# Moving the first GLA head's turn, diagonal and later steps two positions later in a hybrid decoder block

## The chip, the cores and the metric

The kernel runs on one core of a Trainium2 chip. The core has five engines with a queue of instructions each: TensorE (PE in the profile, with its weight loads as PEld), VectorE (DVE), ScalarE (ACT), GpSimd (POOL) and SyncE (SP, which issues most transfers). An engine runs its queue in order; a tie between engines is a semaphore. The metric is the device time of one execution in microseconds; the median of three runs counts.

## The reference

One layer of a decoder: a mixer with two branches, and a gated feed-forward net with a causal convolution, in float32. 16 learned tokens stand ahead of the 1024 of the input, so T = 1040; the model is 1024 wide.

```python
proj = h @ w_in + b_in
# branch 1, GLA: 4 heads, keys and queries 128 wide, values 256 wide, per chunk:
bc = cumsum(log_a)
inter = (q * exp(bc)) @ S
scores[t, s] = sum_k q[t, k] * k[s, k] * exp(bc[t, k] - bc[s, k])      # s <= t
out = inter + scores @ v
S = exp(bc_last) * S + (k * exp(bc_last - bc)).T @ v
# branch 2, mLSTM: 4 heads, the same shape with scalar gates and a running maximum
y = sigmoid(gate_a) * (o_gla @ w_branch_gla) + sigmoid(gate_b) * (o_ml @ w_branch_ml)
h = h + y @ w_out, then the feed-forward net
```

## The kernel before

Products of the projections are split: weights and activations are each held as a high and a low part (wH, wL and xH, xL), and one product is three passes. Weight blocks are loaded into wr, rounded to wH on ACT and subtracted to wL on DVE (both L111 and L112, called a weight split here).

The first third of the kernel is the mixer. Its main stream is a row of projections: for every head the keys and queries (L195, three products of some 342 columns each, "thirds"), then the values (L238: pv_0 for the 16 learned tokens at L225, and pv_1 to pv_8 of 24 products, "blocks"). After head 7 come merge gates (gb). The stream runs through `main`. Beside it run the heads: `gla(s)` for heads 0 to 3 and `mlstm(s)` for heads 4 to 7, one after another in the list `side`, and `post(s)`, which flips a finished head, in the list `closing`. Each `yield` of the stream, one per block or third, adds 1.15 to a sum, and for every whole 1 in it `advance` lets each of the two lists run on to its own next `yield`. So the yields in `gla` say beside which block a piece of it is written; a yield more moves that piece and everything later on the side, the heads after it too. All of `gla` of head 0 but its first levels stands beside the values of head 0 and the keys and queries of head 1.

The written order is a wish: a planner puts the instructions of each engine in a row by their priorities and by when it takes their inputs to be ready. Evictions and weight splits have a higher priority (`hp`). `tc.issue_after(x)` ties instructions behind x, on the same engine's queue where both are there.

The steps of `gla` in order, with the names in the profile. `level(b)`: products of keys and queries with decays over spans of b (pk; exponential on ACT at L786), summed to sc_b on PE (L737, L708 for b = 1) and written to the score tile A by DVE (L754). `diagonal`: kq on DVE (L713), split on ACT (L701) and DVE (L702). `turn`: a product with the flip matrix turns half of A, sct (L727), and ACT copies it to An (L728). `scores_diagonal`: column sums of kq, sc_0 (L708), written by DVE (L721). `scores_large`: sc_32 and sc_64 (L737), written by ACT (L747). Then kh (L819 to L822: difference on DVE, exponential on ACT, product on DVE), qh (L834, L835), the transposes k0t and kt (L840 to L849), the next head's decay (`decay`: pre on PE at L668, la on ACT, bc with a scan on DVE at L681), u and up (L867, L860: state updates), omp, and four output products op (L898 with A or An, L899 with the state S), the states S_0 to S_6 made on DVE (L894).

PSUM, the memory that PE writes, has few buffers here: three named "s" shared by sc, sct, pre, k0t, kt, u, up and the flips ot and otm, three named "pj" shared by the projections, and two for op and omp. A product that takes a buffer waits until its last content has been read.

Of the kernel before, what the change touches and what calls it, by code (L numbers as in the profile page):

```python
# [17 lines left out]
P = 128  # L18
# [4 lines left out]
NK = D // P  # L23
# [4 lines left out]
DV = 256  # L28
# [17 lines left out]
def hybrid_kernel(ctx, tc, x, meta, norm_mix, w_in, b_in, gla_w_gate, gla_b_gate, gla_norm,  # L46
                  ml_conv_w, ml_conv_b, ml_norm, w_branch_gla, w_branch_ml, w_out, norm_ffn,
                  ffn_w_up, ffn_conv_w, ffn_conv_b, ffn_w_down, norm_final, out):
    nc = tc.nc
# [9 lines left out]
    def hp(n):  # L59

        return tc.high_priority(offset=max(1, min(n, tc.cur_priority - floor[0])))
# [140 lines left out]
    def together(*gens):  # L202
        gens = list(gens)
        while gens:
            for g in list(gens):
# [4 lines left out]
                    continue  # L210
                yield

    def proj_v(us, bB, vt):

        for u in us:
            U.get(u)
        for c in range(NC + 1):
            t0 = 0 if c == 0 else NM + P * (c - 1)
            n = NM if c == 0 else P
            pt = ps.tile([P, 512], F32, name=f"pv{us[0]}_{c}", tag="pj", bufs=3)  # L220
            i = 0
            if c == 0:
                for k in range(NK):
                    for b in U.got[us[k // 4]]:
                        nc.tensor.matmul(pt[:, :DV], xM[:, 48 * k:48 * k + P], b[:, k % 4, :],  # L225
                                         start=(i == 0), stop=(i == 2 * NK - 1))
                        i += 1
                with hp(PRI_E):
                    lo = hd.tile([NM, DV], F32, name=f"vlo{us[0]}", tag="junk", bufs=1)
                    nc.scalar.activation(lo, pt[32:48, :DV], AF.Copy)  # L230
                    nc.vector.tensor_tensor(lo, pt[:NM, :DV], lo, OP.add)
                    nc.vector.tensor_tensor(vt[:NM, 0, :DV], lo, bB[:NM, :], OP.add)
                yield
                continue
            for k in range(NK):
                wH, wL = U.got[us[k // 4]]
                for a, b in ((xH, wH), (xH, wL), (xL, wH)):
                    nc.tensor.matmul(pt[:, :DV], a[:, k, t0:t0 + P], b[:, k % 4, :],  # L238
                                     start=(i == 0), stop=(i == 3 * NK - 1))
                    i += 1  # L240
            with hp(PRI_E):
                nc.vector.tensor_tensor(vt[:n, c, :DV], pt[:n, :DV], bB[:n, :], OP.add)  # L242
            yield
# [212 lines left out]
    def key_query_proj(s):  # L456
        h = s % 4
        hh = heads.setdefault(s, {})
        if s < 4:
            pk = key_proj(s) if s != 1 else iter(())  # L460
            qT = hh["q"] = hd.tile([P, T + 3], F32, name=f"qT{s}", tag="q", bufs=2)
            pq = proj_cm(uq[s], TH_POST if s else SEG_POST, T0, lambda p, t0, n: nc.scalar.activation(
                qT[:, t0:t0 + n], p, AF.Identity, bias=cc(C_GQ + h), scale=QS))
            if s == 0:
                k1 = key_proj(1)
                yield from islice(together(pk, pq, k1), 6)
                yield from small_proj()
                token_sums(0, nc.sync)
                pkq = together(pk, pq)
                yield from islice(pkq, 1)  # L470
                decay(0)
                pack()
                yield from pkq
                side.append(gla(0))
                yield from k1
            else:
                yield from pk
                yield from pq
        else:
            kT = hd.tile([P, T + 3], F32, name=f"kT{s}", tag="k", bufs=2)  # L480
            qT = hd.tile([P, T + 3], F32, name=f"qT{s}", tag="q", bufs=2)
            hh["k"], hh["q"] = kT, qT
            for z, u, c in ((kT, uk[s], C_MK), (qT, uq[s], C_MQ)):
                nc.gpsimd.memset(z[:, 0:3], 0.0)
                yield from proj_cm(u, TH_ALL, 0, lambda p, t0, n, z=z, c=c: nc.scalar.activation(
                    z[:, 3 + t0:3 + t0 + n], p, AF.Identity, bias=cc(c + h)))

    def value_proj(s):
        bB = hd.tile([P, DV], F32, name=f"bB{s}", tag="bB", bufs=2)
        nc.sync.dma_start(bB, rowb(b_in, (O_GV if s < 4 else O_MV) + DV * (s % 4), DV))  # L490
        vt = hd.tile([P, NC + 1, DV + 1], F32, name=f"v{s}", tag="v", bufs=2)
        if s >= 4:
            nc.gpsimd.memset(vt[:, :, DV:DV + 1], 1.0)
        heads[s]["v"] = vt
        yield from proj_v(uv[s], bB, vt)
# [188 lines left out]
    def gla(s):  # L684
# [20 lines left out]
        def column_sums(pt, hl):  # L705

            for i, x in enumerate(hl):
                nc.tensor.matmul(pt.rearrange("p i n -> p (i n)"), ones, x, start=(i == 0), stop=(i == 1))  # L708

        def diagonal(g):  # L710

            k, q = (x.rearrange("p (i c t) -> p c i t", c=2, t=P)[:, g] for x in (kv, qv))
            nc.vector.tensor_tensor(raw.rearrange("p (i t) -> p i t", t=P), k, q, OP.mult)  # L713
            return split_raw(f"kq{s}_{g}")

        def scores_diagonal(kq):

            for g in range(2):
                pt = ps.tile([P, 4, P], F32, name=f"sc{s}_0_{g}", tag="s", bufs=3)
                column_sums(pt, kq[g])  # L720
                nc.vector.copy_predicated(An if g else A.rearrange("p (i c) t -> p i c t", c=2)[:, :, 0, :],  # L721
                                          lmask[0][:, None, :].to_broadcast([P, 4, P]), pt)

        def turn():

            pt = ps.tile([P, 4, P], F32, name=f"sct{s}", tag="s", bufs=3)
            nc.tensor.matmul(pt, flip, A.rearrange("p (i c) t -> p i c t", c=2)[:, :, 1, :], start=True, stop=True)  # L727
            nc.scalar.activation(An, pt, AF.Copy)  # L728
# [11 lines left out]
        def scores_large(pk, b):  # L740
            m = 64 // b
            pt = products(pk, b)
            for c in range(2):
                A2 = An if c else A.rearrange("p (i c) t -> p i c t", c=2)[:, :, 0, :]
                for n in range(m):
                    p0 = b * (m * c + n)
                    nc.scalar.activation(A2[2 * b * n:2 * b * n + b, :, 2 * b * n + b:2 * b * (n + 1)],  # L747
                                         pt[p0:p0 + b, :, p0:p0 + b], AF.Copy)
# [55 lines left out]
        with tc.issue_after(placed.ins) if placed else nullcontext():  # L804
            kq = [diagonal(0)]
        kq.append(diagonal(1))
        c, pk = made.pop(0)
        assert c == 32
        turn()
        yield  # L810
        scores_diagonal(kq)
        scores_large(pk, 32)
        (_, pk), = made
        yield
# [499 lines left out]
    def prod3(u, X, kouter, name, ahead=2, base=0):  # L1314
        wH, wL = U.get(u, ahead)
        pt = ps2.tile([P, 3, 512], F32, name=name, tag="big", bufs=2)
        XH, XL = X
        order = [(k, i) for k in range(NK) for i in range(3)] if kouter else [(k, i) for i in range(3) for k in range(NK)]
        for k, i in order:
            t0, n = TH_POST[i]  # L1320
            for a, b, j in ((wH, XH, 0), (wH, XL, 1), (wL, XH, 2)):
                nc.tensor.matmul(pt[:, i, :n], a[:, k, :], b[k][:, base + t0:base + t0 + n],  # L1322
                                 start=(k == 0 and j == 0), stop=(k == NK - 1 and j == 2))
        return pt[:, :, :342]
# [12 lines left out]
    for j in END:  # L1337
        pt = prod3(ugb[j], [[t[:, k] for k in range(NK)] for t in (xH, xL)], False, f"pe{j}", 0, T0)
# [12 lines left out]
    for j in range(NK):  # L1351
# [4 lines left out]
        pt = prod3(ubg[j], og, j < 2, f"bg{j}")  # L1356
# [17 lines left out]
    for j in range(NK):  # L1374
# [7 lines left out]
        pt = prod3(ubm[j], om_, j < 1, f"bm{j}")  # L1382
# [24 lines left out]
    for t in range(NC + 1):  # L1407
        a = r2.tile([P, T], F32, name=f"h{t}", tag=f"Y{t - 1}") if t else rb.tile([P, T], F32, name="h0", tag="T12")
# [222 lines left out]
    def po_bank(n, t, tag):  # L1631
        return psF.tile([P, 512], F32, name=f"po{n}_{t}", tag=tag)
# [5 lines left out]
    for i, tiles in enumerate(([1, 5, 2, 6, 0], [3, 7, 4, 8])):  # L1638
        for n in range(4):
# [13 lines left out]
            for it, t in enumerate(rest):  # L1653
                pt = po_bank(n, t, ("V1", "X1")[it % 2])
# [295 lines left out]
    i = FIRST  # L1950
    while i < len(seq):
        r, ph, m = seq[i]
        k = i % NP2
# [56 lines left out]
```

## Time and profile before

| | |
|---|---|
| median of 3 runs | 1873.1 us (1871.23 to 1874.72) |
| profiled execution | 1872.98 us, span 1871.3 us |
| mean granted clock of PE | 0.997 |
| PE busy | 99% of the span |
| DVE, ACT, POOL busy | 66%, 46%, 22% |
| DMA | 270 MB, 144 GB/s on average |

A row of the timeline gives the start in us, the length in us, the engine, the line and the operation with its tiles; the number behind x says how many instructions the row groups, and a bracket holds the idle time of the engine ahead of it and what ended that. The start of a PE row is where its first product began; products overlap, so the pitch from row to row is what counts, not the length. Head 0's turn is at 92 us, head 1's decay at 109 us, head 1's turn at 164 us, the last flips at 618 us.

### The profile page before, as it was taken

How to read it: one execution, taken by the hardware profiler on the slowest of the kernel's cores; microseconds unless marked ns; L12 is line 12 of the kernel's file. 1: busy time of each engine (PE TensorE's matmuls, PEld its weight loads, DVE VectorE, ACT ScalarE, POOL GpSimd, SP SyncE). 2: the span in 40 equal slices, each digit the busy share in tenths (PEclk: the TensorE clock that was granted, in tenths of full speed). 3: DMA queues.
4: the chain of work that ended last, by engine and by line, in shares of the span. 5: the costliest groups of instructions: out<-in, count | busy, mean ns of one | idle time of the engine just before them, and what ended most of it. 6: DMA issues, size and time to landing. Idle time of an engine off the chain costs nothing. (4 is left out here: it accounts for less than half of the span.)

```text
span 1871.3 us, 32608 instructions
## 1 busy us (share of the span) xinstructions
PE 1848.7 (99%) x13284; PEld 1771.3 (95%) x13284; DVE 1226.0 (66%) x1813; ACT 869.8 (46%) x1395; POOL 420.0 (22%) x476
## 2 busy tenths in 40 slices
PE   8999999999999999999999999999999999999998
PEld 7899999999999999999999999999999999987886
DVE  7766757554563466655532547698787788787876
ACT  6455555545454433432422335543443443465664
POOL 5201101205442000133281600012322222200100
PEclk9999999999999999999999999999999999999999
DMA  5111022143323855565973733334333334288894
GB/s 176 52 37 60 23 61 60 30 122 118 94 78 112 213 136 147 155 185 154 335 242 108 246 132 124 123 88 130 118 103 113 106 104 130 85 319 318 287 382 166
DMA packets 221600, 270.08 MB, mean 144 GB/s; under 512 B 13870, under 2 KB 176737, under 8 KB 221451
## 3 DMA queue, kind: packets, MB, share of 16 engines
q1 hardware_dynamic: 200603, 196.76, 34.0%
q0 software_dynamic: 18336, 62.56, 10.1%
q10 hardware_dynamic: 2512, 8.68, 1.2%
q8 instruction: 104, 1.70, 0.4%
q14 instruction: 45, 0.37, 0.1%
HBM read 198.36 MB, written 69.60 MB: 143 GB/s over the span
## 5 line engine op out<-in xcount | busy, mean ns | idle before, releaser
L546 POOL TENSOR_TENSOR ts<-ts 128x256 f32<-128x256 f32 x88 | 76.7, 877 | 45.2 <-DMA ts<-in_ffn_w_down_dram 43.3
L1529 POOL TENSOR_TENSOR SB<-SA,rg 128x512 f32<-128x512 f32 x20 | 32.7, 1635 | 240.0 <-issue 101.4
L238 PE MATMUL pv<-wH_mv,xH 128*128 128x256 f32 x256 | 74.8, 292 | 0.1
L238 PE MATMUL pv<-wH_gv,xH 128*128 128x256 f32 x256 | 74.6, 291 | 0.0
L788 POOL TENSOR_TENSOR pk<-pk,kT 128x256 f32<-128x256 f32 (+1 forms) x24 | 29.4, 1227 | 192.2 <-ACT pk L786 170.6
L1616 PE MATMUL po<-wH_wo,yH 128*128 128x256 f32 x256 | 72.5, 283 | 0.1
L238 PE MATMUL pv<-wH_gv,xL 128*128 128x256 f32 x256 | 72.1, 282 | 0.0
L238 PE MATMUL pv<-wL_gv,xH 128*128 128x256 f32 x256 | 72.1, 281 | 0.0
L1616 PE MATMUL po<-wL_wo,yH 128*128 128x256 f32 x256 | 71.7, 281 | 0.3 <-DVE wL_wo L112 0.3
L238 PE MATMUL pv<-wL_mv,xH 128*128 128x256 f32 x256 | 72.0, 281 | 0.0
L238 PE MATMUL pv<-wH_mv,xL 128*128 128x256 f32 x256 | 71.9, 281 | 0.0
L1616 PE MATMUL po<-wH_wo,yL 128*128 128x256 f32 x256 | 71.8, 281 | 0.0
L1564 DVE SCALAR_TENSOR_TENSOR cv<-u,fc,cv 128x1024 f32<-128x1024 f32 x44 | 65.1, 1482 | 0.4
L1511 POOL TENSOR_TENSOR A<-u2raw,A 128x512 fp32r<-128x512 f32 x20 | 42.5, 2124 | 86.2 <-ACT A L1510 86.2
L1322 PE MATMUL bg<-ogL,wH_bg 128*128 128x342 f32 x192 | 61.5, 320 | 0.0
L1322 PE MATMUL bg<-ogH,wH_bg 128*128 128x342 f32 x192 | 61.5, 320 | 0.0
L1322 PE MATMUL bm<-omH,wH_bm 128*128 128x342 f32 x192 | 61.4, 320 | 0.0
L1322 PE MATMUL bm<-omH,wL_bm 128*128 128x342 f32 x192 | 61.3, 319 | 0.0
L1322 PE MATMUL bg<-ogH,wL_bg 128*128 128x342 f32 x192 | 61.3, 319 | 0.0
L1322 PE MATMUL bm<-omL,wH_bm 128*128 128x342 f32 x192 | 61.2, 319 | 0.0
L242 DVE TENSOR_TENSOR v<-pv,bB 128x256 f32<-128x256 f32 x64 | 26.5, 418 | 39.2 <-PE pv L238 38.9
L1510 ACT ACTIVATE HA<-rg 128x1024 fp32r<-128x1024 f32 x16 | 17.0, 1060 | 73.0 <-PE Yu L1083 72.6
(787 smaller groups left out, 7523.0 us busy)
## 6 DMA issues: line engine op xcount, KB each, us to landing
gw<-in_w_in_dram SPq DMA_DIRECT2D x26, 512.0 KB
ts<-in_ffn_w_down_dram POOLq DMA_DIRECT2D x44, 256.0 KB, 3.9
tdn<-ts POOLq DMA_DIRECT2D x44, 256.0 KB, 3.1
rg<-in_ffn_w_up_dram SPq DMA_DIRECT2D x22, 512.0 KB
ru<-in_ffn_w_up_dram SPq DMA_DIRECT2D x22, 512.0 KB
adr<-s SPq DMA_DIRECT2D x40, 256.0 KB
rd<-in_ffn_w_down_dram SPq DMA_DIRECT2D x20, 512.0 KB
do<-tdn SPq DMA_DIRECT2D x18, 512.0 KB
```

Of the source, the lines that this page charges most:

```text
L238: nc.tensor.matmul(pt[:, :DV], a[:, k, t0:t0 + P], b[:, k % 4, :], start=(i == 0), stop=(i == 3 * NK - 1))
L242: nc.vector.tensor_tensor(vt[:n, c, :DV], pt[:n, :DV], bB[:n, :], OP.add)
L546: nc.gpsimd.tensor_tensor(t[:, o], t[:, a], t[:, b], OP.subtract)
L788: eng.tensor_tensor(e, e, k, OP.mult)
L1322: nc.tensor.matmul(pt[:, i, :n], a[:, k, :], b[k][:, base + t0:base + t0 + n], start=(k == 0 and j == 0), stop=(k == NK - 1 and j == 2))
L1510: nc.scalar.activation(h, src, AF.Copy)
L1511: eng.tensor_tensor(l, src, h.bitcast(F32), OP.subtract)
L1529: late.tensor_tensor(sb[:, 0:4], sa[:, 0:4], rg[:, 0:4], OP.subtract)
L1564: nc.vector.scalar_tensor_tensor(y, u[:, j:SEQ + j], fc[:, j, jj:jj + 1], y, OP.mult, OP.add)
L1616: nc.tensor.matmul(pt[:, :DV], a, b[:, k % 4, :], start=(k == 0 and i == 0), stop=(k == NK - 1 and i == len(terms) - 1))
```

## The change

`gla` of head 0 gets two yields ahead of the turn. `proj_v` keeps the last product it has written in `filled`, and for head 0 the turn and the diagonal's sums are tied behind the product that was last at that moment. For the heads after it nothing is changed in the code, but the two positions carry through the list to all of them. The instructions of every engine are the same set as before; lines behind the first edit have numbers higher by 2, behind the second by 7.

```diff
+    filled = []
     def proj_v(us, bB, vt):
...
-                    nc.tensor.matmul(pt[:, :DV], a[:, k, t0:t0 + P], b[:, k % 4, :],
-                                     start=(i == 0), stop=(i == 3 * NK - 1))
+                    filled[:] = [nc.tensor.matmul(pt[:, :DV], a[:, k, t0:t0 + P], b[:, k % 4, :],
+                                                  start=(i == 0), stop=(i == 3 * NK - 1)).ins]
...
         kq.append(diagonal(1))
         c, pk = made.pop(0)
         assert c == 32
-        turn()
-        yield
-        scores_diagonal(kq)
+        if s == 0:
+            yield
+            yield
+        with tc.issue_after(filled[0]) if s == 0 else nullcontext():
+            turn()
+        yield
+        with tc.issue_after(filled[0]) if s == 0 else nullcontext():
+            scores_diagonal(kq)
         scores_large(pk, 32)
```

First place, PE at head 0's turn. Before, from the last product of block 5:

```order
L238 MATMUL pv_5_1092<-wH_gv_1_608,xL 128x256
L727 MATMUL sct_1126<-A,flip 128x512
L708 MATMUL sc_0_0_1129<-kq_0_1119,ones 128x512 x2
L708 MATMUL sc_0_1_1133<-kq_1_1123,ones 128x512
L238 MATMUL pv_6_1146<-wH_gv_0_602,xH 128x256
L238 MATMUL pv_6_1146<-wL_gv_0_603,xH 128x256
L737 MATMUL sc_32_1137<-pk_32_1010 128x128 x4
L238 MATMUL pv_6_1146<-wH_gv_0_602,xL 128x256
L708 MATMUL sc_0_1_1133<-kq_1_1123,ones 128x512
```

After, from the last product of block 6, with block 7 cut out between its first and its last product:

```order
L240 MATMUL pv_6_1126<-wH_gv_1_608,xL 128x256
L729 MATMUL sct_1152<-A,flip 128x512
L240 MATMUL pv_7_1155<-wH_gv_0_602,xH 128x256
...
L240 MATMUL pv_7_1155<-wH_gv_1_608,xL 128x256
L710 MATMUL sc_0_0_1181<-kq_0_1119,ones 128x512 x2
L710 MATMUL sc_0_1_1185<-kq_1_1123,ones 128x512 x2
L739 MATMUL sc_32_1189<-pk_32_1010 128x128 x4
L240 MATMUL pv_8_1198<-wH_gv_0_602,xH 128x256
```

The turn has moved behind block 6, and the sums and sc_32 behind block 7, no longer among products of a block.

The same place on ACT. Before:

```order
L701 ACTIVATE kq_0_1119<-An_847 128x512
L701 ACTIVATE kq_1_1123<-An_847 128x512
L728 ACTIVATE An_847<-sct_1126 128x512
L834 ACTIVATE qh_1217<-bc_724 128x1024
L747 ACTIVATE A<-sc_32_1137 32x4x32 x2
L747 ACTIVATE An_847<-sc_32_1137 32x4x32 x2
L821 ACTIVATE kh_1172<-kh_1172 128x1040
```

After:

```order
L703 ACTIVATE kq_0_1119<-An_847 128x512
L703 ACTIVATE kq_1_1123<-An_847 128x512
L828 ACTIVATE kh_1224<-kh_1224 128x1040
L730 ACTIVATE An_847<-sct_1152 128x512
L841 ACTIVATE qh_1276<-bc_724 128x1024
L749 ACTIVATE A<-sc_32_1189 32x4x32 x2
L749 ACTIVATE An_847<-sc_32_1189 32x4x32 x2
```

The exponential of kh now stands ahead of the copy of the turn.

Second place, DVE at head 0's first state update (pre, la and bc are head 1's decay, wL_gk is the low part of a weight block, om belongs to the learned tokens' output). Before:

```order
L677 TENSOR_SCALAR bc_1274<-pre_694_1272 128x346
L680 TENSOR_TENSOR la_1267<-bc_1274,la_1267 128x1040
L894 SCALAR_TENSOR_TENSOR S_0_1365<-S_1320,dl_1182,up_0_1322 128x256
L681 SCALAR_TENSOR_TENSOR bc_1274<-rmask,la_1267 128x1040
L894 SCALAR_TENSOR_TENSOR S_1_1367<-S_0_1365,dl_1182,up_0_1322 128x256
```

After:

```order
L679 TENSOR_SCALAR bc_1333<-pre_694_1331 128x346
L682 TENSOR_TENSOR la_1326<-bc_1333,la_1326 128x1040
L683 SCALAR_TENSOR_TENSOR bc_1333<-rmask,la_1326 128x1040
L112 TENSOR_TENSOR wL_gk_1408<-wr_gk_1405,wH_gk_1407 128x1024
L885 COPY om_1377<-omp_1381 2x256
L901 SCALAR_TENSOR_TENSOR S_0_1391<-S_1372,dl_1234,up_0_1374 128x256
```

S_0 has moved behind the scan, a weight split and the copy of om. On PE, u, up_0, omp, up_1 and the first three products of op_0 stand one behind another there, after the last third of head 1's queries, where thirds stood between them before; pre stands between the second and the last third.

Third place, the end of the merge gates, ACT's queue (of are the flips' copies, gHA the first weight of the next stage, gb a merge gate). Before:

```order
L500 ACTIVATE gb_6182<-pj_342_6215 128x342
L639 ACTIVATE of_0_6241<-ot_0_0_6242,col 128x512
L639 ACTIVATE of_0_6241<-ot_0_1_6248,col 128x512
L1143 ACTIVATE gHA_0_6350<-gw_6346 128x1024
L500 ACTIVATE gb_6182<-pj_684_6258 128x342
L639 ACTIVATE of_1_6284<-ot_1_0_6285,col 128x512
```

After:

```order
L502 ACTIVATE gb_6173<-pj_342_6215 128x342
L1150 ACTIVATE gHA_0_6350<-gw_6346 128x1024
L502 ACTIVATE gb_6173<-pj_684_6241 128x342
L641 ACTIVATE of_0_6267<-ot_0_0_6268,col 128x512
L504 DMA gscb<-gb_6173 128x1026
L641 ACTIVATE of_0_6267<-ot_0_1_6275,col 128x512
L641 ACTIVATE of_1_6285<-ot_1_0_6286,col 128x512
```

The copies of the first half, ahead of the weight before, stand behind it and the last gate now; on PE all of the last head's flips stand behind the last third, where the first half stood ahead of that third.

## The prediction

> **What bounds the kernel now.** I read the engines' share first, then PE's waits, the timeline around the longest of them, and the granted clock there.
>
> ```profile
> PE 1848.7 (99%) x13284; PEld 1771.3 (95%) x13284; DVE 1226.0 (66%) x1813; ACT 869.8 (46%) x1395; POOL 420.0 (22%) x476
> ```
>
> PE is busy 99% of the span and the others far less. No work is added or removed, so the time can only move by what PE waits and by the clock it gets. PE's waits (us in total, times, longest):
>
> ```profile
> PE xtp L358 <- DVE xt L353: 3.5, 3, 2.9
> PE sct L727 <- DVE A L754: 2.7, 2, 2.3
> PE op L899 <- DVE S L894: 0.8, 1, 0.8
> PE sc L708 <- ACT kq L701: 0.7, 1, 0.7
> ```
>
> The first is the start-up, which is not touched. The second and fourth are head 0's turn and diagonal, the third is head 1's first output. The place of the second, PE alone (start, us, instruction, wait):
>
> ```profile
> 89.29 0.28 PE L238 MATMUL pv<-wH_gv,xL 128*128 128x256 f32 x1
> 91.90 1.78 PE L727 MATMUL sct<-A,flip 128*128 128x512 f32 x2 [2.33 <-DVE A L754]
> 95.55 0.80 PE L708 MATMUL sc<-kq,ones 128*128 128x512 f32 x1 [0.68 <-ACT kq L701]
> 99.11 0.28 PE L238 MATMUL pv<-wL_gv,xH 128*128 128x256 f32 x1
> ```
>
> Block 5 ends at 89.29 and the next steady product stands at 99.11. Between them lie the turn, four column sums, sc_32 and four products. The clock, in stretches of 3.41 us (PE busy is the second figure, PEclk the eighth column, after POOL):
>
> ```profile
> 88.83:92.24 3.41, 1.08 (x8) 0.83 (x7) 2.84 (x6) 1.06 (x1) 1.77 (x1) 1.00 0.00 0
> 92.24:95.65 3.41, 2.73 (x5) 0.67 (x3) 2.60 (x5) 1.38 (x3) 0.00 (x0) 0.50 0.00 0
> 95.65:99.06 3.41, 3.41 (x14) 3.22 (x15) 1.82 (x3) 1.94 (x4) 0.00 (x0) 0.50 0.00 0
> 191.23:194.64 3.41, 2.65 (x14) 2.06 (x13) 3.39 (x7) 1.15 (x5) 0.00 (x0) 1.00 0.00 0
> ```
>
> After a stretch with PE busy for 1.08 of 3.41 us (32%) the clock is 0.50 for two stretches; after one with 2.65 (78%) it stays 1.00. The Trainium skill, "TensorE: Matmul & The Clock Gate", section "HAM oscillation — how this bites in real kernels", asks only that no idle gap exceed some 3.4 us; this trace disagrees, for here a gap of 2.33 us is followed by half speed.
>
> **Part 1, the turn and the diagonal behind blocks 6 and 7: a gain.** What the same work takes at full speed shows in head 1:
>
> ```profile
> 163.75 1.02 PE L727 MATMUL sct<-A,flip 128*128 128x512 f32 x2
> 164.77 0.32 PE L195 MATMUL pj<-xL,wH_gk 128*128 128x348 f32 x1
> 168.44 1.10 PE L708 MATMUL sc<-kq,ones 128*128 128x512 f32 x4
> 169.37 1.05 PE L737 MATMUL sc<-pk 128*128 128x128 f32 x8
> 170.18 0.40 PE L195 MATMUL pj<-xH,wH_gk 128*128 128x346 f32 x1
> 102.28 0.36 PE L238 MATMUL pv<-wH_gv,xH 128*128 128x256 f32 x1
> 105.20 0.27 PE L840 MATMUL k0t<-ident,kh 128*16 128x128 f32 x1
> ```
>
> The turn is under 1.02 with one product in it, about 0.86; the sums 169.37 - 168.44 = 0.93; sc_32 170.18 - 169.37 = 0.81; a block of 24 products 105.20 - 102.28 = 2.92, so one is 0.12. Together 0.86 + 0.93 + 0.81 + 5 x 0.12 = 3.2, with a little at each switch 3.5. From 89.29 to 99.11 passed 9.82. The loss is 6.3: waits 2.33 + 0.68, and half of the 2.73 + 3.41 that PE was busy at 0.50, 3.1. Now block 6 stands behind block 5, so PE comes to the turn at 89.41 + 2.85 = 92.3, and A is there (next fence: 91.14 + 0.71 = 91.85). The wait goes with 0.4 to spare, and nothing is left to lower the clock at that place. Gain 6.3; bounds 5.9 (0.4 of wait stays) and 6.6.
>
> **Part 2, the copy of the turn behind the keys' exponential: a cost.** sc_32 takes the PSUM buffer that the turn filled, so it waits for ACT's An<-sct (L728). Before, ACT ran that ahead of qh and kh; now kh's exponential L821 stands ahead of it, and that needs L820, which DVE does behind L819 and the second kq.
>
> ```profile
> 91.14 0.71 DVE L754 COPY_PREDICATED A<-mu,sc 128x512 f32<-128x512 uint8 x1
> 95.01 1.22 DVE L819 TENSOR_TENSOR kh<-bc 128x1024 f32<-128x1024 f32 x1
> 96.14 0.69 DVE L702 TENSOR_TENSOR kq<-An,kq 128x512 fp32r<-128x512 f32 x1
> 99.87 0.15 DVE L820 TENSOR_TENSOR kh<-bc 128x16 f32<-128x16 f32 x1
> 95.53 0.60 ACT L728 ACTIVATE An<-sct 128x512 f32<-128x512 f32 x1
> 100.58 1.07 ACT L821 ACTIVATE kh<-kh 128x1040 f32<-128x1040 f32 x1
> 101.68 1.24 DVE L822 TENSOR_TENSOR kh<-kh,kT 128x1040 f32<-128x1040 f32 x1 [0.53 <-ACT kh L821]
> 96.74 0.73 DVE L721 COPY_PREDICATED A<-mu,sc 128x512 f32<-128x512 uint8 x1
> ```
>
> DVE's order up to the second kq is the old one, so that still ends at 96.83, L820 at 96.9, L821 at 98.0, the copy at 98.6. PE: turn until 93.15, block 7 until 96.05, the sums wait some 0.1 for the second kq and end at 97.1. sc_32 waits 98.6 - 97.1 = 1.5. Bounds: 0.7 if kh's chain runs one DVE instruction of 0.69 sooner, 2.2 if later by as much. I take 1.6 with the sums' 0.1. Until the copy, qh and the fills of sc_32 are late too; sc_64, a block later (98.6 + 0.8 + 2.9), finds its buffer read by then, since L822 and the two L721 behind the exponential take 1.24 + 2 x 0.73 from 98.0.
>
> **Part 3, head 0's first state update behind head 1's scan: a cost.** The decay products L668 move from ahead of all three query thirds to between the second and third. DVE then meets the scan L681 and the weight split wL_gk ahead of S_0, where S_0 stood ahead of the scan. Head 1 has this order already, but for the split:
>
> ```profile
> 183.85 0.64 PE L668 MATMUL pre<-raw_s,wgp 81*128 81x348 f32 x3
> 190.53 2.32 DVE L681 TENSOR_TENSOR_SCAN bc<-rmask,la 128x1040 f32<-128x1040 f32 x1
> 193.09 0.46 DVE L894 SCALAR_TENSOR_TENSOR S<-S,dl,up 128x256 f32<-128x256 f32 x1
> 193.60 0.70 PE L899 MATMUL op<-S,qh 128*128 128x256 f32 x2 [0.76 <-DVE S L894]
> 127.65 1.22 DVE L112 TENSOR_TENSOR wL_gk<-wr_gk,wH_gk 128x1024 fp32r<-128x1024 f32 x1
> 128.79 0.48 DVE L894 SCALAR_TENSOR_TENSOR S<-S,dl,up 128x256 f32<-128x256 f32 x1
> ```
>
> There PE was ready 193.60 - 0.76 - 183.85 = 9.0 after the decay products and S came at 9.75. The split adds 128.79 - 127.65 = 1.1: wait 0.76 + 1.1 = 1.9. Bounds 0.76 (the split costs nothing) and 2.3 (0.4 more for om, L878). On ACT the split's other half, wH_gk, waits for the last query product and is done before the scan is. Head 1 itself now has its 16 products of value block 0 (1.9 us) between, and a split of its own ahead of the scan: its 0.76 becomes some 0.4, bounds 0 and 0.8.
>
> **Part 4, the last head's flips: a cost.** Before, the first half stood ahead of the last merge-gate third and only the second half behind it. Now all stand behind it, and ot_1_0 needs the buffer of ot_0_0, which ACT reads behind a weight copy and a gate:
>
> ```profile
> 618.19 1.04 PE L637 MATMUL ot<-ident,or 128*128 128x128 f32 x8
> 619.30 0.42 PE L195 MATMUL pc<-xH,wH_gb 128*128 128x342 f32 x1
> 618.23 1.06 ACT L1143 ACTIVATE gHA<-gw 128x1024 fp32r<-128x1024 f32 x1 [3.16 <-PE pj L195]
> 619.20 0.44 ACT L500 ACTIVATE gb<-pj 128x342 f32<-128x342 f32 x1
> 619.53 0.68 ACT L639 ACTIVATE of<-ot,col 128x512 f32<-128x512 f32 x1
> ```
>
> PE has done three flips 619.30 - 618.19 = 1.1 after the third's end; ACT's read is done 619.53 + 0.68 - 618.19 = 2.0 after. Cost 0.9, bounds 0 (ACT takes the read first) and 1.3 (the next flip waits too).
>
> **The rest of the move.** Everything later on the side (levels of heads 1 to 3, all of heads 4 to 7, the flips) comes two positions later. Head 1 then stands about as head 2 stood, head 2 as head 3, where the waits list above has nothing but 0.4 at head 3's turn (2.7 - 2.3), so I put these at 0, bounds -0.4 and +1. On SP the stores of finished heads stand behind weight loads, and POOL's queue changes by three rows; no listed wait of PE names either, cost 0.
>
> **Sum.** -6.3 + 1.6 + 1.9 - 0.4 + 0.9 = -2.3, best -6.6 + 0.7 + 0.8 - 0.8 - 0.4 = -6.3, worst -5.9 + 2.2 + 2.3 + 1.3 + 1 = +0.9. The profiled execution took 1872.98 (span 1871.3 and 1.7 around it), 0.1 below the median 1873.1. So 1870.7, between 1866.7 and 1873.9 with the clock full.
>
> **Rivals.**
> *The new waits halve the clock.* Part 2 leaves PE busy 1 - 1.6/3.41 = 53% of a stretch, part 3 leaves 44%. The trace has 32% halved and 78% kept, so the limit may lie on either side; and a wait may be cut in two by a stretch's border. One halving costs about the 3.1 of part 1: 1873.8. Both: 1876.9, slower than before; it decides once the limit lies above 53% and each wait falls within one stretch. By the skill's rule of 3.4 us neither wait would halve the clock, and the time would stay 1870.7.
> *The new waits are smaller.* If ACT and DVE get the copy and S_0 done in time, parts 2 and 3 go to their lower bounds and the time is 1867 to 1869. Against it: both waits follow from an order of instructions on one engine, which cannot be overtaken.
> *The change does not do what it says.* The turn still waits for A, if A's chain is later than 92.3: at most the margin's loss, some 1 us, 1871.7. The rows of DVE up to A are in the old order, so I think it unlikely.
> *A level of head 1 or 2 comes late.* With two more weight splits (1.22 each) ahead of the last level in head 1, its turn could wait 2 us and halve the clock: 1870.7 + 2 + 3.1 = 1875.8. A of head 1 in the kernel before:
>
> ```profile
> 159.59 0.72 DVE L754 COPY_PREDICATED A<-mu,sc 128x512 f32<-128x512 uint8 x1
> ```
>
> It was done at 160.3 and the turn came at 163.75, so there is room of 3.4 us for two splits.
>
> **How the numbers follow.** As worked, clock full: 0.42. New waits smaller: 0.19. The turn still waits: 0.03. One halving: 0.14. Both: 0.12; a late level with its halving: 0.10. About 0.2% (3.7 us) is what a measurement of this kernel can tell from no change: faster means under 1869.4, slower over 1876.8. The first case lies mostly inside (0.06 of it below), the second below, the third and fourth inside; the last two lie about the upper border, 0.2 of their 0.22 above once something else goes wrong with them. Faster 0.25, same 0.55, slower 0.20. Leaving out one in ten at each end gives 1867.3 to 1877.5.
>
> **What would show it.** Right: no wait at the turn, PEclk 1.00 from 88 to 100; sc_32 waiting 1.5 for ACT's An; op's second S product waiting 1.9 at head 0; ot_1_0 waiting 0.9. Wrong: PEclk 0.50 behind either wait, or a wait in heads 1 to 3 that this list lacks.

## The result, and the profile after

The changed kernel takes 1882.3 us (median of five runs, 1882.1 to 1884.1) against 1873.1 (1871.2 to 1874.7): ratio 1.0052, 95% interval 1.0041 to 1.0063. The forecast was 1870.7 within 1867.3 to 1877.5, so it is outside, on the slow side. The profiled execution, with a span of 1882.4 us against 1871.3, is the slowest of the five; the medians lie 9.2 us apart, the two traces 11.1.

PE's waits after (us in total, times, longest):

```profile
PE u L997 <- ACT of L641: 7.6, 1, 7.6
PE xtp L360 <- DVE xt L355: 3.4, 3, 2.8
PE sc L739 <- ACT An L730: 2.2, 2, 1.5
...
PE op L906 <- DVE S L901: 1.7, 1, 1.7
PE sc L739 <- ACT of L641: 1.2, 1, 1.2
...
PE ot L639 <- ACT of L641: 0.9, 1, 0.9
...
PE pj L195 <- DVE v L244: 0.7, 1, 0.7
```

The wait at head 0's turn is gone, the expected new waits (sc at An, op at S, ot at of) are there, and the list is headed by one that the forecast did not have: u, the first state product of head 7, waits 7.6 us for a copy of head 6's flips. At that place (POOL, ACT and PE of the timeline, in order of time):

```profile
569.15 0.40 PE L195 MATMUL pj<-xH,wH_gb 128*128 128x342 f32 x1
569.39 1.51 POOL L542 DMA_DIRECT2D ts<-in_ffn_w_down_dram  x2
573.44 0.60 PE L639 MATMUL ot<-ident,or 128*128 128x128 f32 x4
575.64 0.72 POOL L548 TENSOR_TENSOR ts<-ts 128x256 f32<-128x256 f32 x1 [4.74 <-DMA ts<-in_ffn_w_down_dram]
579.76 0.69 POOL L550 DMA_DIRECT2D tdn<-ts  x1 [0.30 <-POOL ts L548]
582.60 0.46 ACT L502 ACTIVATE gb<-pj 128x342 f32<-128x342 f32 x1 [12.79 <-DMA tdn<-ts]
582.95 0.68 ACT L641 ACTIVATE of<-ot,col 128x512 f32<-128x512 f32 x1
583.78 1.19 PE L997 MATMUL u<-v,K 16*128 16x257 f32 x2 [7.60 <-ACT of L641]
```

ts is a background tile: beside the last heads POOL loads a part of the next stage's down weights into it, makes sums and stores them as tdn. It has the name "gst" and a single buffer, and the first merge gate gb takes the same buffer. So ACT's first copy of gb cannot start before the store of ts has landed, 582.6; ACT had been idle for 12.79 us. Behind it on ACT stands the copy of the flip (ot of 573.44), and u needs the PSUM buffer that this copy frees. The same places before:

```profile
563.82 1.45 POOL L540 DMA_DIRECT2D ts<-in_ffn_w_down_dram  x2
571.50 0.69 POOL L548 DMA_DIRECT2D tdn<-ts  x1 [0.30 <-POOL ts L546]
571.59 0.70 PE L990 MATMUL u<-v,K 16*128 16x257 f32 x2
572.57 0.51 PE L195 MATMUL pj<-xH,wH_gb 128*128 128x342 f32 x1
576.77 0.46 ACT L500 ACTIVATE gb<-pj 128x342 f32<-128x342 f32 x1 [3.75 <-PE pj L195]
```

There ACT waited for the projection and not for ts, and the flips' copies and u stood ahead of gb. The load has moved from 563.82 to 569.39, while the merge gate's first third, which belongs to the main stream, has not moved with it: it starts 3.4 us sooner, at 569.15 instead of 572.57, as less of the heads' work stands ahead of it. What starts the load is the end of head 6:

```profile
546.52 1.86 POOL L95 TENSOR_TENSOR rs6r<-rs6v,mhalf 128x9 f32<-128x9 f32 x1 [24.64 <-DVE rs6v L93]
```

is the row before, and the row after is:

```profile
553.10 1.83 POOL L95 TENSOR_TENSOR rs6r<-rs6v,mhalf 128x9 f32<-128x9 f32 x1 [28.20 <-DVE rs6v L93]
```

From there POOL runs sums of the tokens, their stores, and then the load, in both kernels. The load also took longer: POOL waited 4.74 us for it where it had waited 2.17 (the first of the tile's four sums began at 567.44 before and at 575.64 after).

The granted clock after, in stretches of 3.41 us (PE busy is the second figure, the clock stands after POOL):

```profile
96.54:99.95 3.41, 1.79 (x11) 1.08 (x10) 2.53 (x7) 2.58 (x3) 0.00 (x0) 0.99 0.00 0
99.95:103.36 3.41, 3.41 (x19) 3.41 (x18) 2.42 (x4) 1.30 (x6) 0.00 (x0) 0.51 0.00 0
123.84:127.25 3.41, 2.06 (x15) 2.01 (x16) 2.85 (x8) 1.89 (x7) 0.00 (x0) 1.00 0.44 125
577.77:581.18 3.41, 0.00 (x0) 0.00 (x0) 0.00 (x0) 0.00 (x0) 2.39 (x4) 1.00 0.28 97
581.18:584.60 3.42, 0.82 (x2) 0.50 (x2) 0.00 (x0) 1.03 (x2) 0.00 (x0) 0.50 0.21 74
584.60:588.01 3.41, 3.41 (x11) 2.93 (x11) 0.48 (x1) 0.39 (x1) 0.00 (x0) 0.50 0.34 138
```

The clock is halved behind sc_32's wait for one stretch (3.41 of busy PE, 1.7 lost) and behind u's for two (4.2 busy, 2.1 lost). All of the difference lies ahead of the next stage, whose first product pc stood at 619.30:

```profile
630.58 0.42 PE L195 MATMUL pc<-xH,wH_gb 128*128 128x342 f32 x1
```

630.58 - 619.30 = 11.3 us, where the spans differ by 11.1. Some 0.3 of it lies ahead of the change already, for the start-ups of two executions are not alike. Where traces are compared closely below, pc is therefore counted from the last level's sum ahead of head 0's turn, which all kernels share. Before and after:

```profile
85.68 1.05 PE L737 MATMUL sc<-pk 128*128 128x128 f32 x8
85.94 1.05 PE L739 MATMUL sc<-pk 128*128 128x128 f32 x8
```

From there to pc it is 533.6 us before and 544.6 after, 11.0 more.

### The profile page after: what moved, and what is told of

Same layout as the page of the kernel before. It is cut to its first block, busy times and chain, and to the rows that moved or that the text cites. A ratio compares the mean times of both kernels' runs of the same rounds, so it can differ in the third digit from the quotient of the medians.

```text
span 1882.4 us, 32597 instructions
## 1 busy us (share of the span) xinstructions
PE 1849.5 (98%) x13284; PEld 1772.8 (94%) x13284; DVE 1222.6 (65%) x1813; ACT 869.3 (46%) x1395; POOL 423.8 (23%) x476
## 4 chain that ended last, share of the span: by engine, by line
PE 81%; DVE 6%; DMA 4%; issue 4%; POOL 2%; ACT 2%; SPq 0%; POOLq 0%; ACTq 0%; DVEq 0%
PE pj L195 8%; PE Yu L1090 6%; PE Xu L1090 6%; PE Zu L1090 6%; PE pv L240 6%; PE bg L1329 5%; PE bm L1329 5%; PE Zg L1090 4%; PE Yg L1090 4%; PE Xg L1090 4%; PE po L1623 4%; PE Vu L1090 3%; PE pdX L1780 2%; PE pdZ L1780 2%; PE pdY L1780 2%
```

## The experiments

Times are medians beside runs of the kernel before on the same chip (1872.4 for e1 to e4, 1872.7 for e5 to e8); ratios are against those.

**e1, the background tile in another buffer.** "bc" is a single buffer too; it held the decays of heads 0 and 2, and after them the convolved queries qc of heads 4 to 7 lie in it.

```diff
-                                t = half_load(wp, "gst")
+                                t = half_load(hd, "bc") if s == 6 else half_load(wp, "gst")
```

> The changed kernel, with one thing other: head 6's background tile (ts of the down weights' sums, filled and emptied by POOL and its DMAs) lies in a buffer of its own kind that the GLA heads have left, and no longer in the single buffer that the merge gate's gb takes. The order of every engine is that of the changed kernel. Theory (the merge gate's first copy waits for that buffer, and u behind it for ACT): u's wait of 7.6 us and the half clock behind it (4.2 us of busy PE at 0.50, 2.1) go, 1882.3 - 9.7 = 1872.6. Rival (u waits because the heads' flips come too late for PSUM, whatever the buffer of gb): u still waits over 5 us, 1880 to 1882. Rival (the loss is at head 0, by its new waits and the clock): 1881 to 1882.

Measured 1873.6, ratio 1.0005 (0.9996 to 1.0015). u does not wait any more:

```profile
PE xtp L360 <- DVE xt L355: 3.5, 3, 2.9
PE sc L739 <- ACT An L730: 1.9, 2, 1.2
...
PE op L906 <- DVE S L901: 1.7, 1, 1.7
PE sc L739 <- ACT of L641: 1.2, 1, 1.2
```

The buffer is not one of the tile's own, as was expected: the load waits on POOL for 7.35 us, until head 7's products with qc (msc) have read it (the last ends at 573.50), and starts at 574.09. So the tile's last store is issued even later than in the changed kernel (579.76), and u runs at 573.43 without waiting for it:

```profile
573.43 0.70 PE L997 MATMUL u<-v,K 16*128 16x257 f32 x2
581.40 0.70 POOL L550 DMA_DIRECT2D tdn<-ts  x1 [0.30 <-POOL ts L548]
```

No engine's order was changed and no instruction left out, so gb's sharing of the buffer is the cause of u's wait, and with the clock behind it of about 9 us of the median. Both rivals fall: the flips stand where they stood in the changed kernel, and the new waits at head 0 are still there. One thing more differs in this trace, which the buffer does not explain: sc_32 waits 1.2, not 1.5, and the clock behind it stays full (1.7). From the last level's sum (84.94) to pc (618.27) it is 533.3 us, 0.3 less than before.

**e2, heads 4 to 7 put back.** The small rows' step between heads 3 and 4 has six empty yields; four are left.

```diff
-        for _ in range(6):
+        for _ in range(4):
             yield
         for g in range(3):
```

> The changed kernel, with two of six empty yields taken out of the small rows' step that stands between head 3 and head 4, so that heads 4 to 7 and their flips stand where they stood before the change, while heads 0 to 3 stay two positions later. Theory: everything of the loss that lies in heads 4 to 7 goes (7.6 + 2.1 at u, 0.9 at the last flips, 0.7 at head 4's keys), 1882.3 - 11.3 = 1871.0. Rival (the loss is at head 0 and in heads 1 to 3): 1880 to 1882.

Measured 1880.4, ratio 1.0038 (1.0023 to 1.0053): a miss. u's wait is gone as the theory has it, but two new ones have come, with two stretches of half clock beside them (385.04 to 391.87):

```profile
PE rtp L611 <- DVE of L653: 4.3, 1, 4.3
...
PE rtp L611 <- ACT of L641: 1.7, 1, 1.7
```

rtp are the small rows' transposes, which now meet a GLA head's late flips; the row of DVE ahead of that copy says what held it:

```profile
387.15 0.17 DVE L957 COPY gp<-WB 128x8 f32<-128x8 f32 x1 [7.16 <-DMA WB<-rsc]
388.66 0.21 DVE L653 TENSOR_SCALAR of<-otm,col 128x2 f32<-128x2 f32 x1
388.93 1.12 PE L611 MATMUL rtp<-ident,srst 128*128 128x128 f32 x4 [4.29 <-DVE of L653]
```

DVE stood 7.16 us at a load of head 4 (WB) with the flip's copy behind it. In the changed kernel DVE stands at the same load, for 7.72 us, but there the transposes come at 393.7, when the copy is done. The six yields stand ahead of the transposes, and with four of them the transposes come too soon. As a test of where the loss lies the run says only that u's wait goes with the late heads' place.

**e3, only heads 4 to 7 later.** The kernel before with eight yields in that step; head 0 is as it was.

> The kernel before, with two more empty yields in the small rows' step, so that only heads 4 to 7 stand two positions later, and head 0's turn is where it was. Theory: the whole loss without the gain, 1873.1 + 7.6 + 2.1 + 0.9 = 1883.7. Rival (the loss is at head 0 and in heads 1 to 3): 1873 to 1874.

Measured 1886.5, ratio 1.0067 (1.0052 to 1.0082), 2.8 more than the 1883.7 of the theory; in the trace u waits 1.3 longer than in the changed kernel, and the half clock behind it lasts three stretches instead of two, 0.8 more. The waits:

```profile
PE u L990 <- ACT of L639: 8.9, 1, 8.9
...
PE sct L727 <- DVE A L754: 2.2, 2, 1.8
...
PE ot L637 <- ACT of L639: 0.9, 1, 0.9
```

Head 0's old wait and its half clock stay, and the late heads alone bring u's, here 8.9. So the loss needs nothing of what was done at head 0's turn: the two positions, handed down the list to head 6, are enough.

**e4, head 0's copy of the turn first on ACT.**

```diff
+            copied[:] = [nc.scalar.activation(An, pt, AF.Copy).ins]
...
+        with tc.issue_after(copied[0]) if s == 0 else nullcontext():
             nc.scalar.activation(kh, kh, AF.Exp, scale=1.0 / 16)
```

> The changed kernel, with head 0's exponential of kh tied behind the copy of the turn on ACT, as those two stood before the change. If sc_32's wait of 1.5 us and the stretch of half clock behind it (3.4 us of busy PE at 0.50, 1.7) both come from that order: 1882.3 - 3.2 = 1879.1, and the clock is 1.00 from 95 to 106 us. If the half clock comes from something else: 1880.8.

Measured 1882.9, ratio 1.0052 (1.0037 to 1.0067): no gain over the changed kernel. Yet at head 0 it did what was expected, sc_32 waits no more and the clock is full there. Head 7's transposes, ahead of u, show it: in the changed kernel and in e4

```profile
568.41 0.27 PE L964 MATMUL k0t<-ident,kc 128*16 128x128 f32 x1
```

```profile
565.35 0.27 PE L966 MATMUL k0t<-ident,kc 128*16 128x128 f32 x1
581.37 1.19 PE L999 MATMUL u<-v,K 16*128 16x257 f32 x2 [8.26 <-ACT of L641]
```

3.06 us earlier, of 3.2 expected. At u 0.7 of it is given back, as its wait is now 8.26, and about 0.7 more, as the half clock behind it lasts three stretches (576.73 to 586.97, 5.6 us of busy PE) instead of two. So pc stands 1.8 earlier than in the changed kernel (628.79); the span is 0.7 shorter. Where the rest went behind pc is not settled: from pc to the end it is 1251.8 us in the changed kernel, 1252.9 in e4 and 1254.0 in e1, with no change there. The median shows no gain at all.

**e5, the buffer, the copies first in heads 0 to 2, and S_0 first.** e1 and e4's tie (for s < 3), and a priority for head 0's first state:

```diff
+                    with hp(3000) if s == 0 and c == 0 else nullcontext():
                         nc.vector.scalar_tensor_tensor(Sn[:, :DV], S[:, :DV], dl[:, c:c + 1], up[:, i, :], OP.mult, OP.add)
```

> The kernel with the background tile in a buffer of its own (e1), and two of the new waits taken away by order: in heads 0 to 2 the exponential of kh stands behind the copy of the turn on ACT, and head 0's S_0 is given a higher priority, which puts it ahead of the scan and of the weight split on DVE. Theory (with the buffer out of the way, what is left of the loss are the small new waits): sc_32's 1.2 and 0.7 (heads 0 and 2) and S_0's 1.7 go, e1's 1873.6 - 3.6 = 1870.0. Rival (such waits are only handed on): 1873 to 1874, as e1.

Measured 1870.1, ratio 0.9989 (0.9980 to 0.9998), faster than the changed kernel and, by 0.1%, than the kernel before. sc's wait for An is gone and S's is down to 0.4:

```profile
PE sc L739 <- ACT of L641: 1.2, 1, 1.2
...
PE op L909 <- DVE S L904: 0.4, 1, 0.4
```

From the last level's sum (85.35) to pc (615.49) it is 530.1 us, 3.2 less than in e1, and the waits are shorter by 1.2 + 0.7 + 1.7 - 0.4 = 3.2: with the buffer out of the way the small waits are worth their length, and are not handed on.

**e6, e5 and the next stage's weight copy behind the last flips.**

```diff
+            with tc.issue_after(flipped[7]) if 7 in flipped else nullcontext():
+                nc.scalar.activation(h, src, AF.Copy)
+            flipped.pop(7, None)
```

> e5, and ACT's first weight copy of the next stage, gHA, behind the copies of the last flips. If the last flips' 0.9 is worth its length: 1870.0 - 0.9 = 1869.1, with pc's first product 0.9 earlier than in e5. If gHA's products wait for it instead: 1870 to 1871.

Measured 1869.8, ratio 0.9986 (0.9977 to 0.9995), against e5 within the noise. ot's wait is down from 0.9 to 0.3, but pc stands at 615.69, not earlier than in e5: a wait of pj for kT has grown by as much (1.0 against 0.4), and from the last level's sum (84.94) pc comes 0.6 later, which is not explained. A product of the next stage (Xg) waits 1.4 us anew. So this small wait was not worth its length.

**e7, only head 6's flips later.** The kernel before, with five yields in place of three ahead of head 6's flips.

```diff
-        for _ in range(3 if s != 3 else 6):
+        for _ in range(5 if s == 6 else 3 if s != 3 else 6):
```

> The kernel before, with only head 6's flips two positions later. On POOL nothing changes its place: token sums, load, sums and stores of the background tile stand as before. Theory (the late thing is the background tile, whose chain hangs on head 6's end): u does not wait, 1872 to 1873. Rival (the flips are what comes too late for u's PSUM buffer): u waits 5 us or more, 1880.

Measured 1873.4, ratio 1.0006 (0.9997 to 1.0015), and u does not wait. Late flips of head 6 alone do not bring the wait. The run does not repeat the changed kernel's order, though: u stays at 571.48, ahead of gb (576.67) and of the last flip. That the late background tile is the cause is what e1 shows; in the changed kernel the flip's copy stands behind gb and gb needs the buffer.

**e8, one position instead of two.**

```diff
         if s == 0:
             yield
-            yield
```

> The changed kernel with one empty yield in place of two. Head 0's turn then still stands behind block 5, so its wait of 2.3 us stays, while everything later stands one position later. Theory: before, the buffer was free at 574.3 and wanted at 576.8, 2.5 us to spare; after, two positions, it was late by 7.6 (10.1 in all). One position takes about half of that: u waits some 2.5 us, 1872.4 + 2.5 = 1875. Rival (the loss grows with the turn's place): 1872.4.

Measured 1879.5 (1875.6 to 1880.2), ratio 1.0034 (1.0021 to 1.0046). The direction is the theory's, the size is above it. The trace is of the fastest execution, 1875.57; the other four took 1879.1 to 1880.2. In it the turn's wait is still there (1.8), and the buffer's takes another form:

```profile
571.44 0.69 POOL L550 DMA_DIRECT2D tdn<-ts  x1 [0.30 <-POOL ts L548]
577.35 0.46 ACT L502 ACTIVATE gb<-pj 128x342 f32<-128x342 f32 x1 [9.95 <-DMA tdn<-ts]
577.70 0.38 ACT L998 ACTIVATE C<-u 128x257 f32<-128x257 f32 x1
578.13 0.83 PE L1025 MATMUL op<-C,WB 128*128 128x257 f32 x2 [3.22 <-ACT C L998]
```

Here u had run, and it is the state C, copied by ACT behind gb, that PE waits for. The store took 577.35 - 571.44 = 5.9 us to free the buffer, against 582.60 - 579.76 = 2.8 in the changed kernel. How late the buffer comes is thus a matter of the transfers beside it too; in the trace two weight blocks had been issued at 566.68.

That this execution took what the theory said is luck: the wait at C costs 3.2 and a stretch of half clock 1.7, a flip at 306.5 waits 2.4 anew, and against that the turn's wait of 1.8 did not halve the clock (the second row is the stretch behind it):

```profile
87.05:90.46 3.41, 1.64 (x14) 1.43 (x13) 2.84 (x6) 1.06 (x1) 1.65 (x1) 1.00 0.00 0
90.46:93.87 3.41, 3.40 (x23) 2.92 (x24) 2.60 (x5) 1.06 (x2) 0.12 (x1) 1.00 0.00 0
```

In the kernel before the half clock there cost 3.1. Had the other four paid it, that would be some 1878.7, near where they lie; no trace shows them.

**The ties.** The ties behind a block's last product do nothing here: the kernel built without them has row for row the changed kernel's order on every engine, and built with them but without the two yields it has that of the kernel before. The two yields are the whole change.

## Why the prediction was wrong

**The step that failed** is "The rest of the move": "Head 1 then stands about as head 2 stood, head 2 as head 3 [...] so I put these at 0, bounds -0.4 and +1", and in it "POOL's queue changes by three rows; no listed wait of PE names either, cost 0". The heads were compared with each other, which is right for what moves together. But the main stream does not move with the heads, and at its end the moved work meets it: the background tile of head 6 lies in the one buffer that gb takes. That no wait was listed before meant that there was room, and the room was not worked out. Before, the buffer was free at some 571.50 + 2.8 = 574.3 and wanted at 576.77, so 2.5 us. After, it was wanted at some 573.7 (the third ends at 573.44, and in e1 the copy follows 0.25 behind) and free at 582.60, 8.9 late. Of these 11.4 us the load's later start is 5.6, its slower landing 2.6, and the gate that came sooner 3.1; without the slow landing two positions are 8.7, and one, half of that, is already more than the room. That POOL's order is hardly changed says nothing of when its instructions run. The term, put at 0, measured 7.6 of wait and 2.1 of half clock (e1: about 9 of the median's time), and 2.2 from heads 2 to 4 (new waits of 0.7, 1.2 and 0.7 less head 3's old 0.4). The first two of these are waits in heads 1 to 3 of the kind that the prediction named as a sign of being wrong.

**Part 1, the turn: right in place, a little large.** No wait at the turn, and no half clock until 99.95. The three terms that the prediction lists for the loss add up to 2.33 + 0.68 + 3.1 = 6.1; its 6.3 is what is left of 9.82. e1 measures the gain: its new waits (1.2 + 0.7 + 1.7 + 1.2 + 0.9 + 0.7, and 0.3 of pj for kT) less the 0.76 and 0.35 of before are 5.5, and pc still comes 0.3 sooner than before, so the gain is some 5.8, just under the lower bound of 5.9.

**Part 2, sc_32: right in cause and size**, 1.49 against 1.5:

```profile
97.34 1.07 ACT L828 ACTIVATE kh<-kh 128x1040 f32<-128x1040 f32 x1 [1.52 <-DVE kh L827]
98.44 0.60 ACT L730 ACTIVATE An<-sct 128x512 f32<-128x512 f32 x1
99.18 1.39 PE L739 MATMUL sc<-pk 128*128 128x128 f32 x8 [1.49 <-ACT An L730]
```

The bounds left out that it can halve the clock, which stood in a rival with 0.14.

**Part 3, S_0: right**, 1.66 against 1.9; head 1's own wait left the list instead of falling to 0.4.

**Part 4, the last flips: right**, 0.89 against 0.9.

**The rivals.** One halving came at sc_32, as the first rival had it, with half its price (one stretch, 1.7, in place of 3.1). At S_0, with PE busy for 2.06 of 3.41, the clock stayed. The prediction looked for a limit between 32% and 78% of a stretch, and the traces show no sharp one: it was halved behind stretches with PE busy for 1.08 (before), 1.61 (e3, at the turn) and 1.79 (after, at sc_32), but it stayed behind 1.64 (e8, at the turn), 1.76 (e4, at S_0) and 1.81 (after, ahead of u's wait), and behind every stretch at full clock with 2.0 or more. The stretches are laid by each trace's own clock changes. So PE's busy time in a stretch is not the whole of what decides. The rival on a late level asked the right question, whether a step comes too late for the main stream, of the wrong place.

## What to carry to other kernels

Where a change moves a chain of work against a stream that stays, look for every buffer that both use, and work out for each when it is freed and when it is wanted: the room is in no list of waits, and it can be less than the shift. A queue whose order is unchanged still moves in time with what starts it. A gain at one place can be lost again at a wait downstream that is set by something else (e4); take such a wait away first (e1), then small ones can be worth their length (e5), though not each is (e6). And two traces are compared from a point that both share behind the start-up, not from 0.

## What the runs showed of the hardware that was not expected

The same background load held POOL for 2.17 us before and 4.74 after, and one store freed its buffer after 2.8 us in one kernel and after 5.9 in another. Beside the longer load two weight blocks had just been issued:

```profile
569.10 1.85 SPq L107 DMA_DIRECT2D wr_gb<-in_w_in_dram  x2
```

The other traces agree with that. In the changed kernel, e3 and e4 the load was issued 0.3 us behind these two blocks, and it took 6.2, 7.2 and 6.8 us from issue to landing; in the seven other traces, where no block was issued in the 3 us ahead of it, it took 3.2 to 3.8. e8's stores were issued 3.0 and 4.8 us behind the blocks and took 6.4 in the median, against 2.5 to 2.8 elsewhere. No run moved the weight blocks alone, so it is likely and not shown that they slow the others.

And a wait of PE can halve the clock in one execution and not in another: the turn's wait of 1.8 us did so in e3 and did not in e8.
